# Output projection among the recurrence steps, with its sums in DRAM, in a one-layer hybrid decoder step

## The chip, the cores and the metric

The kernel runs on one core of one Trainium2 chip. The metric is the device time of one execution in microseconds (us). Times shown as "start" in rows of the trace count from the first instruction of the profiled execution.

## What is computed

One decoder layer for 1,024 prompt tokens and 8 decode tokens, width 1,024. The projected row is split: 512 channels go through a pooling mixer in 4 groups of 128, the rest through RWKV-7 with 8 heads of 64. Both results, side by side, go through one output projection.

```python
h = _rmsnorm(x, norm1_g)
proj = h @ w_in                                     # 1024 -> 512 + 1792
pool_out = _pool_mixer(proj[..., :512], ...)        # window means minus token, 128x128 map per group
# RWKV-7, per head, token by token:
sa = einsum('bhvk,bhk->bhv', S, -kk)
S = S * decay + sa (kk * a) + v k                   # state update
y = einsum('bhvk,bhk->bhv', S, r)                   # then group norm, bonus, gate
mix = concatenate([pool_out, rwkv_out]) @ w_out     # 1024 -> 1024
x = x + mix
h2 = _rmsnorm(x, norm2_g)
x = x + square(relu(h2 @ w_up)) @ w_down            # 1024 -> 4096 -> 1024
```

The final norm, the new states and the pooling and shift buffers are outputs too.

## The kernel before

**Layout.** Everything is transposed: channels on the 128 partitions, tokens along the free axis. The tokens stand in two halves (512, and 512 + 8 decode tokens); each half has two segments of 256. A full-precision product is made of three matmuls on split operands (`gemm`, L183): high by high, high by low, low by high. `weights` (L155) loads a weight tile `wr` on GpSimd's DMA queue (4 buffers) and splits it into `wh` and `wl` on ScalarE and VectorE (6 buffers each).

**Stages.** `token_block` builds the normed input of a segment (`xh`, `xl`, 2 buffers: segment 2 reuses those of segment 0). `project` makes one of 18 row blocks `pj` of the input projection: 0 to 3 are the pool groups, 4 to 15 r, k and v of the four head pairs, 16 and 17 the low-rank inputs. `stage1` (S) makes the chunk matrices of a head pair and half, and writes `sc`, `bkt`, `vt`. `inverse` (I) inverts the 64 by 64 chunk matrices of two head pairs over one segment, with two trips through DRAM (`blk`, `inv`, `Dg`, `TX`). `chain` (C) then steps the state through the segment's four chunks (`pcs`, L588 to L599), norms and gates the output (`py`, L622) and stores it to DRAM (`mix`). There are eight units S0 to S7 (four head pairs, two halves) and eight blocks I0 to I7 and C0 to C7: C0, C1 and C2, C3 are the first half, C4 to C7 the second.

**Pool groups.** `pools` (P) steps `pool_group`: the `pj` products of a group, window sums, then the 128 by 128 map `po` with a weight `pw` from the GpSimd queue. `pw` has one buffer, so that each load waits for the `po` of the group before. The result goes to `mix` in DRAM.

**Order.** The string `ORDER` is the program order: R makes r, k, v, T the token blocks of segments 2 and 3 with block 16's weights, L the second half's low-rank inputs, Q the decode pool rows, D the first part of `decode`. Within it the scheduler orders each engine's instructions by priority (`high_priority`, the LEAD offsets); each engine runs its list in order and waits on semaphores.

**Output projection.** `mixed` reads a `mix` tile back and splits it (`mr`, `mh`, `ml`); `out_block` makes 128 output channels (`mx`) and adds them to `x`. The first half's products are written behind C7 in the program, with priority ahead for C7 (`lead_chain(blocks[7])`), and the decode steps between them. The second half's follow with 7 of 8 k tiles, then `norm2(0)`, then the last k tile among the first `up` products. The MLP (`up`, `dn`) takes the rest.

## Time and profile before

| | |
|---|---|
| runs of before, us | 1369.88, 1372.07, 1374.78 (median 1372.07) |
| profiled execution, us | 1369.46 |
| its span, first to last instruction, us | 1367.7 |
| C0 starts / C7's last `py` / MLP's steady stretch starts, us | 127.3 / 555 / 647.6 |

The profiled execution spends 1.8 us outside its span. PE is TensorE's matmuls; they are pipelined, so the busy time of PE is longer than what it would need at the spacing of its matmuls, and only the spacing tells its load. PEclk is the clock that TensorE was granted, as a share of full speed.

### The profile page before, as it was taken

To read this page: it belongs to the slowest core of one execution; us is meant where nothing else is said; L and a number is where in the kernel's file an instruction comes from. 1 tells how busy PE (TensorE), PEld (TensorE's weight loads), DVE (VectorE), ACT (ScalarE), POOL (GpSimd) and SP (SyncE) were. 2 spreads that over 40 slices of the span, in tenths; PEclk is the share of its full clock that TensorE was granted. 3 is DMA by queue.
4 is the path that set the end of the run, shared out by engine and by line. 5 is a ranking of instruction groups with operands and counts; after the bars stand their busy time and mean duration, and the time that the engine had idled before them with its cause. 6 is when DMAs were issued, how large, how long until landed. Compare 5 with 4: busy or idle time off the path is not lost.

```text
span 1367.7 us, 24214 instructions
## 1 busy us (share of the span) xinstructions
PE 1304.4 (95%) x9748; PEld 1149.8 (84%) x9748; DVE 806.9 (59%) x1782; ACT 555.2 (41%) x1261; POOL 152.2 (11%) x301
## 2 busy tenths in 40 slices
PE   6999996999999899999999999999999999999996
PEld 6988775878877676798999999999999999999986
DVE  7887577747866765748644535445444354453447
ACT  7655766766767667626211212112111121121123
POOL 3112001111100110120010100100000100000000
PEclk9999996999999899999999999999999999999998
DMA  7234123221321542431111111111111111111103
GB/s 226 70 80 115 44 61 74 77 52 54 71 50 42 160 127 79 158 132 60 47 55 39 55 47 40 54 40 47 54 39 55 47 43 50 45 48 48 47 7 124
DMA packets 81647, 94.52 MB, mean 69 GB/s; under 512 B 52504, under 2 KB 58776, under 8 KB 81528
## 3 DMA queue, kind: packets, MB, share of 16 engines
q0 software_dynamic: 20480, 66.04, 15.1%
q1 hardware_dynamic: 59728, 25.10, 7.3%
q8 instruction: 76, 1.25, 0.4%
q10 hardware_dynamic: 1328, 1.85, 0.4%
q14 instruction: 35, 0.29, 0.1%
HBM read 79.67 MB, written 13.51 MB: 68 GB/s over the span
## 4 chain that ended last, share of the span: by engine, by line
PE 77%; ACT 7%; DVE 6%; issue 5%; DMA 3%; POOL 1%; SPq 0%; DVEq 0%; POOLq 0%; ACTq 0%
PE dn L183 26%; PE up L183 26%; PE pj L183 7%; PE mx L183 5%; PE sc L415 2%; PE pcs L599 1%; PE pcs L593 1%; ACT SV L100 1%; DMA cst<-in_consts 1%; ACT TT L100 1%; PE py L589 1%; DVE tm L517 1%; ACT ys L100 1%; PE pcs L588 1%; DVE wl L173 1%
## 5 line engine op out<-in xcount | busy, mean ns | idle before, releaser
L100 ACT ACTIVATE wh<-wr 128x512 fp32r<-128x512 f32 x230 | 143.2, 626 | 357.8 <-PE dn L183 276.2
L183 PE MATMUL up<-h2h,wl 128*128 128x260 f32 (+1 forms) x768 | 245.6, 320 | 0.0
L183 PE MATMUL up<-h2h,wh 128*128 128x260 f32 (+1 forms) x768 | 245.1, 320 | 0.5 <-DVE u L930 0.5
L183 PE MATMUL up<-h2l,wh 128*128 128x260 f32 (+1 forms) x768 | 244.9, 320 | 0.0
L183 PE MATMUL dn<-uh,wl 128*128 128x512 f32 (+1 forms) x720 | 231.0, 321 | 0.0
L183 PE MATMUL dn<-ul,wh 128*128 128x512 f32 (+1 forms) x720 | 230.6, 320 | 0.0
L183 PE MATMUL dn<-uh,wh 128*128 128x512 f32 (+1 forms) x720 | 230.3, 320 | 0.0
L969 DVE TENSOR_TENSOR x<-dn,x 128x260 f32<-128x260 f32 (+1 forms) x192 | 99.1, 516 | 189.6 <-PE dn L183 189.6
L183 PE MATMUL pj<-xh,wh 128*128 128x258 f32 (+3 forms) x576 | 174.8, 303 | 10.8 <-ACT wh L100 9.7
L173 DVE TENSOR_TENSOR wl<-wr,wh 128x512 fp32r<-128x512 f32 x230 | 156.4, 684 | 41.0 <-ACT wh L100 37.6
L183 PE MATMUL pj<-xh,wl 128*128 128x258 f32 (+3 forms) x576 | 172.0, 299 | 0.0
L183 PE MATMUL pj<-xl,wh 128*128 128x258 f32 (+3 forms) x576 | 171.6, 298 | 0.0
L183 PEld LDWEIGHTS up<-h2l,wh 128*128 128x128 f32 x768 | 144.5, 188 | 12.3 <-DVE h2l L912 0.6
L183 PEld LDWEIGHTS up<-h2h,wh 128*128 128x128 f32 x768 | 144.2, 188 | 11.7 <-DVE u L930 0.9
L183 PEld LDWEIGHTS up<-h2h,wl 128*128 128x128 f32 x768 | 144.4, 188 | 11.1
L183 PEld LDWEIGHTS dn<-ul,wh 128*128 128x128 f32 x720 | 135.5, 188 | 10.9 <-issue 0.2
L183 PEld LDWEIGHTS dn<-uh,wh 128*128 128x128 f32 x720 | 135.7, 188 | 10.5
L183 PEld LDWEIGHTS dn<-uh,wl 128*128 128x128 f32 x720 | 135.4, 188 | 10.6 <-issue 0.2
L100 ACT ACTIVATE uh<-u 128x260 fp32r<-128x260 f32 (+1 forms) x96 | 47.2, 492 | 238.6 <-DVE u L931 238.6
L183 PEld LDWEIGHTS pj<-xh,wh 128*128 128x128 f32 x576 | 112.4, 195 | 16.5 <-ACT wh L100 9.7
L930 DVE SCALAR_TENSOR_TENSOR u<-up,rs 128x260 f32<-128x260 f32 (+1 forms) x96 | 49.5, 517 | 120.8 <-PE up L183 114.3
L183 PEld LDWEIGHTS pj<-xl,wh 128*128 128x128 f32 x576 | 112.6, 195 | 3.9 <-issue 2.6
(291 smaller groups left out, 2088.5 us busy)
## 6 DMA issues: line engine op xcount, KB each, us to landing
wr<-in_w_in POOLq DMA_DIRECT2D x72, 256.0 KB, 3.1
wr<-in_w_up POOLq DMA_DIRECT2D x64, 256.0 KB, 2.9
wr<-in_w_down POOLq DMA_DIRECT2D x64, 256.0 KB, 2.9
wr<-in_w_out POOLq DMA_DIRECT2D x26, 256.0 KB, 3.3
xr<-in_xT SPq DMA_DIRECT2D x16, 256.0 KB, 3.7
mr<-mix SPq DMA_DIRECT2D x8, 260.0 KB, 3.5
x<-in_xT SPq DMA_DIRECT2D x2, 1040.0 KB, 7.9
blk<-AA SPq DMA_DIRECT2D x16, 128.0 KB, 2.6
```

The lines of the kernel that those rows point to most:

```text
L100: A.activation(out, in_, func, bias=bias, scale=scale, **k)
L173: V.tensor_tensor(l[:, :w], raw[:, :w], f32(h[:, :w]), op=ALU.subtract)
L183: PE.matmul(ps, lhs, rhs, start=i == 0, stop=i == n - 1)
L415: PE.matmul(scs[h][:, c, :], BK[R[h], c, :, :], AR[R[h], c, :, h, :], start=True, stop=True)
L517: V.tensor_tensor(pr[:, q], l[:, q].unsqueeze(2).to_broadcast([64, m, m, m]), r[:, q].rearrange("p k j -> p j k").unsqueeze(1).to_broadcas ...
L588: PE.matmul(pq[:, u], B.AR[u][:, c, 0, :, :], SV[:, c, u], start=True, stop=True)
L589: PE.matmul(py[u][:, c, :, :], SV[:, c, u], B.AR[u][:, c, 1, :, :], start=True, stop=False)
L593: PE.matmul(pa[:, u], TT[:, 4 * u + c, :, :], Q[:, u], start=True, stop=True)
L599: PE.matmul(pu[:, u], B.BKT[u][:, c, :, :], SV[:, c, u], start=True, stop=True)
L930: V.scalar_tensor_tensor(u, ps[:, :n], 0.0, rs2[:, cs], ALU.max, ALU.mult)
L969: V.tensor_tensor(d, ps[:, :n], d, op=ALU.add)
```

## The change

The program order is rewritten. Parts of the pool groups stand elsewhere, T preloads the weights of row blocks 16 and 17, `project_later` makes both blocks for segment 2 before segment 3 takes part, and four new parts M0 to M3 make output projection: M0 and M1 the whole first half (8 k tiles, right behind S7 and D), M2 and M3 the second half over k tiles 0 to 5. They take `x` from the input, add the product and store the sum to a DRAM tensor `x1_d`. Behind the loop `load_x1` reads all of it back, and the last two k tiles (C6's and C7's heads) are added behind `norm2(0)`.

```diff
-ORDER = """R0 S0 R1 S1 P00 I0 Q P01 C0 I1 P02 C1 R2 S2 R3 T S3 L I2 R4 C2 I3 R5 C3 S4 S5 I4 R6 C4 I5 R7 C5 S6 S7 I6 P10 C6 I7 P11 P12 D"""
+ORDER = """R0 S0 R1 S1 I0 Q R2 C0 I1 R3 P00 P01 P02 T C1 S2 L S3 I2 R4 C2 I3 P10 R5 C3 S4 S5 I4 R6 P11 C4 I5 R7 P12 C5 S6 S7 M0 I6 D M1 C6 I7 M2 M3 C7"""
...
-                GP.dma_start(raw.rearrange("p (m c) -> p m c", c=P), src)
+                GP.dma_start(raw.rearrange("p (m c) -> p m c", c=src.shape[-1]), src)
...
-        with tc.high_priority(offset=LEADX if b > 1 else 0):
+        with tc.high_priority(offset=LEADX if b == 2 else 0):
...
+    def project_later():
+
+        ws = [ahead.pop(m) for m in (16, 17)]
+        for b in (2, 3):
+            next(late.pop(b))
+            if b == 2:
+                next(late[3])
+            for w, (m, use) in zip(ws, hold):
+                project_block(m, w, b, use, 0)
+
+    hold = []
+
     def project(m, half, use):
+        if m > 15 and half:
+            hold.append((m, use))
+            return
...
+        if half:
+            project_later()
         sigm(z0[0:64, :n], z0[0:64, :n], 0.0, 2.0)
...
             next(late[2])
             ahead[16] = weights(I["w_in"][16])
-            next(late[3])
+            ahead[17] = weights(I["w_in"][17])
...
+    x1_d = [dr.tile([P, KT, n], F32, name=f"x1_{i}") for i, (_, n) in enumerate(HALF)]
+    mx = {}
+
+    def mixed_early(half):
+
+        mx[half] = []
+        n = HALF[half][1]
+        for k in range(KT - 2 * half):
+            if k % 4 == 0:
+                h, l = (xp.tile([P, KT, 266], F32R, tag=x, name=f"m{x}{k}_{half}", bufs=NX).rearrange("p k t -> p (k t)")
+                        for x in ("xh", "xl"))
+            c = slice(n * (k % 4), n * (k % 4) + n)
+            raw = big(f"mr{k}_{half}", ("f", "e", "u0", "u1")[k % 4])[:, :n]
+            SY.dma_start(raw, mix_d[k][half])
+            act(h[:, c], raw)
+            V.tensor_tensor(l[:, c], raw, f32(h[:, c]), op=ALU.subtract)
+            mx[half].append((h[:, c], l[:, c]))
+
+    def out_early(m, half):
+
+        c0, n = HALF[half]
+        ops = mx[half]
+        x = big(f"xm{m}_{half}", f"d{m % 2}")[:, :n]
+        SY.dma_start(x, I["xT"][:, m, c0:c0 + n])
+        w = weights(I["w_out"][m, :, :len(ops) * P])
+        for o, q in ((0, 260), (260, 260)) if half else ((0, 512),):
+            ps = ps_d.tile([P, 512], F32, tag="d", name=f"mx{half}_{m}_{o}")
+            gemm(ps[:, :q], w, [(h[:, o:o + q], l[:, o:o + q]) for h, l in ops])
+            V.tensor_tensor(x[:, o:o + q], ps[:, :q], x[:, o:o + q], op=ALU.add)
+        SY.dma_start(x1_d[half][:, m, :], x)
+
+    def outs(part):
+        half, part = part // 2, part % 2
+        if part == 0:
+            if half:
+                for _ in dec[0]:
+                    pass
+            mixed_early(half)
+        for m in range(4 * part, 4 * part + 4):
+            out_early(m, half)
+            if dec:
+                next(dec[0], None)
...
+        elif c[0] == "M":
+            outs(int(c[1]))
...
-            SY.dma_start(x1[half][:, k:k + 4, :], I["xT"][:, k:k + 4, c0:c0 + n])
+            SY.dma_start(x1[half][:, k:k + 4, :], x1_d[half][:, k:k + 4, :])
...
-    lead_chain(blocks[7])
-    open_x1(0)
-    with tc.tile_pool(name="opa", bufs=1, side="right", reuse_waits="tile") as op:
-        ops = [mixed(op, k, 0, NMA) for k in range(KT)]
-        for m in range(KT):
-            out_block(m, weights(I["w_out"][m]), ops, 0, 0, 512)
-            next(dec, None)
-    open_x1(1)
+    for half in range(2):
+        open_x1(half)
+        load_x1(half)
...
-        ops = [mixed(op, k, 1, 3) for k in range(KT - 1)]
-        for m in range(KT):
-            w = weights(I["w_out"][m, :, :(KT - 1) * P])
-            for o in (0, 260):
-                out_block(m, w, ops, 1, o, 260)
         norm2(0, 512, lambda x: op.tile([P, 512], F32, tag="n2", name=x, bufs=2))
-        last = [mixed(op, KT - 1, 1, 3)]
-        w7 = [w for m in (0, 4) for w in weights(I["w_out"][m:m + 4, :, (KT - 1) * P:].rearrange("m p c -> p m c"))]
-        for m in range(KT):
-            for o in (0, 260):
-                out_block(m, w7[m:m + 1], last, 1, o, 260)
+        ops = [mixed(op, k, 1, 3) for k in range(KT - 2, KT)]
+        for m in range(0, KT, 2):
+            w = weights(I["w_out"][m:m + 2, :, (KT - 2) * P:].rearrange("m p c -> p m c"))
+            for i in range(2):
+                for o in (0, 260):
+                    out_block(m + i, w[2 * i:2 * i + 2], ops, 1, o, 260)
```
```

Wide products (`pj`, `mx`, `up`) in the program order of PE between marks of the recurrence; "start" is a block's first `pcs`, "end" its last `py` with `glu`. The other matmuls are left out here.

| stretch of PE's order | before: 512 columns, 256 to 266 columns | after |
|---|---|---|
| program start to C0 start | 0, 649 | 0, 652 |
| C0 start to C1 start | 0, 82 | 0, 92 |
| C1 start to end | 0, 55 | 0, 80 |
| C1 end to C2 start | 0, 276 | 0, 418 |
| C2 start to C4 start | 0, 527 | 0, 441 |
| C4 start to C5 start | 0, 77 | 18, 45 |
| C5 start to end | 0, 53 | 30, 0 |
| C5 end to C6 start | 40, 9 | 141, 0 |
| C6 start to C7 start | 33, 0 | 3, 29 |
| C7 start to end | 41, 0 | 0, 74 |

**Between C1's end and C2's start, GpSimd's queue.** Before, the first half's last pool weights are loaded ahead of the recurrence's first `mix` stores (`pw` is a pool weight, `d` a pool group's result, `ys` the recurrence's output of block C0, `wr` a weight tile).

```order
L751 DMA pw1_0_1247<-in_pool_w 128x128
L776 DMA mix0_0_70<-d0_0_1106 128x512
L165 DMA wr_2349<-in_w_in 128x512
L751 DMA pw2_0_1558<-in_pool_w 128x128
L776 DMA mix1_0_72<-d1_0_1147 128x512
L165 DMA wr_2413<-in_w_in 128x512
L751 DMA pw3_0_1567<-in_pool_w 128x128
L776 DMA mix2_0_74<-d2_0_1409 128x512
L165 DMA wr_2419<-in_w_in 128x512
L399 MEMSET AA1_0_2202 128x16
L751 DMA pw0_1_5500<-in_pool_w 128x128
```

After the change the same loads stand behind C1's stores.

```order
L645 DMA mix4_0_78<-ys0_1_2422 128x256
L645 DMA mix5_0_80<-ys0_1_2422 128x256
L768 DMA pw1_0_2082<-in_pool_w 128x128
L793 DMA mix0_0_70<-d0_0_1941 128x512
L768 DMA pw2_0_2240<-in_pool_w 128x128
L793 DMA mix1_0_72<-d1_0_1982 128x512
L768 DMA pw3_0_2249<-in_pool_w 128x128
L793 DMA mix2_0_74<-d2_0_2091 128x512
L165 DMA wr_2310<-in_w_in 128x512
L165 DMA wr_2316<-in_w_in 128x512
L165 DMA wr_2322<-in_w_in 128x512
L165 DMA wr_2328<-in_w_in 128x512
L793 DMA mix3_0_76<-d3_0_2133 128x512
```

Three `pw` loads, each with a `mix` store of the group before it in line behind, now stand between C1's output and the next four weight loads, which are row blocks 16 and 17 of the second half.

**Between C5's end and C6's start, PE.** Before, the last `bkt` of S7 stands here, followed by `vt`, the start of C6's chunks, and the first pool maps (`po`) and output products (`mx`, of channels 0 and 1).

```order
L427 MATMUL bkt3_3_5193<-cst_86,BK_147 128x128 x4
L441 MATMUL vt1_2_5200<-cst_86,v2_1_4191 128x128 x2
L441 MATMUL vt1_2_5200<-cst_86,v3_1_4664 128x128 x2
L441 MATMUL vt1_3_5210<-cst_86,v2_1_4191 128x128 x2
L441 MATMUL vt1_3_5210<-cst_86,v3_1_4664 128x128 x2
L588 MATMUL pcs_108<-SV1_2_5199,AR0_135 128x128
L589 MATMUL py1_2_0_5517<-AR0_135,SV1_2_5199 128x128
L588 MATMUL pcs_108<-SV1_2_5199,AR1_136 128x128
L589 MATMUL py1_2_1_5518<-AR1_136,SV1_2_5199 128x128
L774 MATMUL po0_1_0_5905<-d0_1_5366,pw0_1_5500 128x256
L774 MATMUL po0_1_256_5908<-d0_1_5366,pw0_1_5500 128x264
L183 MATMUL mx0_0_0_8_6201<-mh0_0_6142,wh_6191 128x512
```

After the change the same `bkt` stands here, among the output products of channel block 4.

```order
L183 MATMUL mx0_4_0_5980<-mxh4_0_5572,wh_5976 128x512
L432 MATMUL sc3_3_0_5512<-AR3_138,BK_147 128x128 x4
L183 MATMUL mx0_4_0_5980<-mxl4_0_5573,wh_5976 128x512
L432 MATMUL sc3_3_1_5513<-AR3_138,BK_147 128x128 x4
L183 MATMUL mx0_4_0_5980<-mxh4_0_5572,wl_5977 128x512
L183 MATMUL mx0_4_0_5980<-mxh4_0_5572,wh_5976 128x512
L444 MATMUL bkt3_3_5528<-cst_86,BK_147 128x128 x4
L183 MATMUL mx0_4_0_5980<-mxl4_0_5573,wh_5976 128x512
L183 MATMUL mx0_4_0_5980<-mxh4_0_5572,wl_5977 128x512
L183 MATMUL mx0_4_0_5980<-mxh4_0_5572,wh_5976 128x512
L183 MATMUL mx0_4_0_5980<-mxl4_0_5573,wh_5976 128x512
L458 MATMUL vt1_2_5535<-cst_86,v2_1_4343 128x128 x2
```

Ahead of this `bkt` and behind C5's end there are now 64 products of 512 columns and all matmuls of S6 and S7, and behind it, up to C6's start, 77 (of before 0 and 40); the pool maps are gone from here.

**Behind C7, SP's queue.** Before, the second half's `mix` tiles are read, and then `x`, in two halves, from the kernel's input.

```order
L869 DMA mr2_1_6705<-mix2_1_75 128x520
L869 DMA mr3_1_6711<-mix3_1_77 128x520
L869 DMA mr4_1_6717<-mix4_1_79 128x520
L869 DMA mr5_1_6723<-mix5_1_81 128x520
L869 DMA mr6_1_6729<-mix6_1_83 128x520
L869 DMA mr7_1_7248<-mix7_1_85 128x520
L855 DMA x11_6672<-in_xT 128x4x520 x2
```

After the change `x` of both halves comes from the sums in DRAM.

```order
L869 DMA xm6_1_6917<-in_xT 128x520
L875 DMA x1_1_458<-xm5_1_6862 128x520
L869 DMA xm7_1_6972<-in_xT 128x520
L875 DMA x1_1_458<-xm6_1_6917 128x520
L919 DMA x11_7150<-x1_1_458 128x2080
L875 DMA x1_1_458<-xm7_1_6972 128x520
L919 DMA x10_7144<-x1_0_457 128x2048 x2
L919 DMA x11_7150<-x1_1_458 128x2080
```

The loads of `x1_1` and `x1_0` stand around and behind the store of the last sum (`xm7`), in the same queue.

## Rows read from the trace of the kernel before

**Rows 1.** The page's first part: busy time of each engine, its share of the span, and its instructions.

```profile
PE 1304.4 (95%) x9748; PEld 1149.8 (84%) x9748; DVE 806.9 (59%) x1782; ACT 555.2 (41%) x1261; POOL 152.2 (11%) x301
```

**Rows 2.** The table by stretches, cut at the marks of the recurrence: start and end, length, busy time (and instructions) of PE, its weight loads, DVE, ACT and POOL, the granted clock, the share of DMA time and GB/s.

```profile
0.00:127.30 127.30, 113.58 (x978) 103.65 (x978) 102.20 (x252) 81.16 (x175) 27.40 (x65) 0.99 0.44 127
127.30:158.90 31.60, 30.44 (x370) 24.68 (x369) 18.22 (x51) 21.88 (x57) 2.67 (x7) 1.00 0.27 66
158.90:185.10 26.20, 25.54 (x176) 21.16 (x175) 19.28 (x52) 18.71 (x44) 0.00 (x0) 1.00 0.01 2
185.10:261.30 76.20, 59.88 (x548) 52.63 (x546) 55.58 (x134) 50.77 (x120) 10.08 (x20) 0.82 0.34 88
261.30:292.10 30.80, 28.95 (x368) 24.26 (x368) 18.30 (x52) 20.62 (x57) 3.05 (x7) 1.00 0.22 57
261.30:393.50 132.20, 125.78 (x1198) 108.60 (x1198) 89.30 (x226) 84.67 (x209) 14.64 (x29) 0.97 0.23 60
393.50:428.50 35.00, 33.04 (x399) 27.43 (x399) 29.40 (x82) 23.56 (x64) 3.35 (x7) 1.00 0.19 50
428.50:454.30 25.80, 25.71 (x166) 20.59 (x165) 18.54 (x47) 19.28 (x45) 2.16 (x4) 1.00 0.12 30
454.30:494.30 40.00, 33.33 (x313) 26.14 (x312) 26.31 (x67) 24.95 (x66) 8.09 (x15) 0.77 0.60 170
494.30:529.80 35.50, 33.36 (x361) 23.68 (x359) 24.08 (x64) 28.76 (x95) 1.98 (x4) 0.97 0.34 106
529.80:556.00 26.20, 25.92 (x158) 19.26 (x158) 12.66 (x31) 15.18 (x47) 3.00 (x7) 1.00 0.19 61
```

**Rows 3.** The timeline of PE at some marks: start, duration, engine, line, tiles, shape and count; in brackets the wait before.

```profile
230.20 1.09 PE L427 MATMUL bkt<-cst,BK 128*128 128x128 f32 x4 [1.05 <-DVE AR L422]
...
261.34 0.71 PE L593 MATMUL pcs<-Q,TT 128*128 128x128 f32 x4
...
362.29 0.60 PE L427 MATMUL bkt<-cst,BK 128*128 128x128 f32 x4
...
393.46 0.71 PE L593 MATMUL pcs<-Q,TT 128*128 128x128 f32 x4
...
460.02 1.09 PE L427 MATMUL bkt<-cst,BK 128*128 128x128 f32 x4 [1.78 <-DVE AR L422]
...
494.27 1.05 PE L593 MATMUL pcs<-Q,TT 128*128 128x128 f32 x4
```

**Rows 4.** The same timeline in two steady stretches of output products, the first and last row of each: 21 matmuls of 512 columns, then 25 of 260; and two neighbouring `py` of four records.

```profile
560.16 0.40 PE L183 MATMUL mx<-mh,wh 128*128 128x512 f32 x1
...
564.79 0.40 PE L183 MATMUL mx<-mh,wl 128*128 128x512 f32 x1
...
587.29 0.28 PE L183 MATMUL mx<-mh,wl 128*128 128x260 f32 x1
...
590.17 0.28 PE L183 MATMUL mx<-mh,wl 128*128 128x260 f32 x1
...
555.04 1.13 PE L622 MATMUL py<-z,glu 128*128 128x256 f32 x4
555.83 0.58 PE L183 MATMUL mx<-mh,wh 128*128 128x512 f32 x1
```

**Rows 5.** PE's waits between 185 and 261: line, releaser, us in total, times, longest.

```profile
PE pb L384 <- DVE bv L382: 5.3, 1, 5.3
PE ss L250 <- DVE acc L234: 4.1, 1, 4.1
PE pk L373 <- ACT w L100: 3.1, 1, 3.1
```

**Rows 6.** POOL's waits in the same stretch, one row of its weight loads.

```profile
POOL wr L165 <- DVE acc L234: 9.6, 4, 4.4
```

**Rows 7.** The table by stretches again, for the granted clock (the number behind POOL's).

```profile
200.00:207.00 7.00, 6.89 (x25) 5.50 (x26) 4.32 (x12) 5.54 (x14) 0.54 (x1) 0.57 0.57 160
213.00:233.00 20.00, 12.72 (x53) 10.17 (x53) 15.27 (x39) 7.18 (x16) 2.15 (x4) 0.50 0.41 95
```

**Rows 8.** The timeline of POOL's queue, pool weights of the second half and the waits before them.

```profile
467.81 0.54 POOL L751 DMA_DIRECT2D pw<-in_pool_w  x1 [8.12 <-PE po L774]
...
472.97 0.54 POOL L751 DMA_DIRECT2D pw<-in_pool_w  x1 [2.98 <-PE po L774]
```

**Rows 9.** All instructions on the tile `pw`: time from issue to landing of its loads.

```profile
DMA to landing us min/median/max: 2.1/2.7/5.8
```

**Rows 10.** The chain that ended last, between 556 and 620: start, duration, work.

```profile
569.54 3.42 DMA mr<-mix
...
583.00 35.41 PE mx L183 x294
```

**Rows 11.** PE's waits between 556 and 648.

```profile
PE mx L183 <- DVE x L880: 1.4, 1, 1.4
PE ss L905 <- DVE acc L903: 0.7, 1, 0.7
```

**Rows 12.** DMA between 555 and 600: GB/s in 40 slices, and issues with count, KB each and the median us to landing.

```profile
GB/s 0 25 259 197 37 145 7 7 144 375 401 202 3 109 257 383 310 59 207 125 323 374 348 403 412 399 382 211 15 0 0 227 181 0 0 98 258 52 15 0
...
mr<-mix SPq DMA_DIRECT2D x8, 260.0 KB, 3.5
x<-in_xT SPq DMA_DIRECT2D x2, 1040.0 KB, 7.9
```

More of the change, by code (lines that the diff above doesn't have):

```diff
@@ L850, in open_x1, with load_x1 @@
     def open_x1(half):
-        c0, n = HALF[half]
+        n = HALF[half][1]
         xq = open_pool(ctx, f"x1{half}", side="right", reuse_waits="tile")
         x1.append(xq.tile([P, KT, n], F32, name=f"x1{half}"))
+    def load_x1(half):
         for k in range(0, KT, 4):
-            SY.dma_start(x1[half][:, k:k + 4, :], I["xT"][:, k:k + 4, c0:c0 + n])
+            SY.dma_start(x1[half][:, k:k + 4, :], x1_d[half][:, k:k + 4, :])
     def x1s(m, c, n):
```

## The prediction

> **What bounds the kernel now.** I began with the page's engine shares: matmuls are busy for 95% of the span, VectorE for 59%, ScalarE for 41% [rows 1]. Busy time of pipelined matmuls says little, so I next read the spacing: 21 products of 512 columns start 4.63 us apart from first to last, 0.231 us each, and 25 of 260 columns 2.88 us, 0.120 us each [rows 4]. Two 256-column matmuls with plain fp32 operands, four records, take 555.04 to 555.83, 0.40 us each [rows 4]; I scale the recurrence's and the inverse's other matmuls from that by width (an estimate). The table by stretches [rows 2] then shows how long each stage takes, and the table of counts in the change's section what PE must do in it. The difference is what I call stall: time above PE's spacing, whether it shows as a wait, as half clock or as gaps of an in-order queue.
>
> | stretch | length before | wide + other work before | stall before | work after |
> |---|---|---|---|---|
> | to C0 | 127.3 | 77.9 + 26.3 | 23.1 | 78.2 + 22.9 |
> | C0 to C1 | 31.6 | 9.8 + 15.1 | 6.7 | 11.0 + 12.5 |
> | C1 | 26.2 | 6.6 + 16.6 | 3.0 | 9.6 + 10.5 |
> | C1 end to C2 | 76.2 | 33.1 + 14.4 | 28.7 | 50.2 + 26.6 |
> | C2 to C4 | 132.2 | 63.2 + 46.7 | 22.3 | 52.9 + 45.9 |
> | C4 to C5 | 35.0 | 9.2 + 18.5 | 7.3 | 9.6 + 16.8 |
> | C5 | 25.8 | 6.4 + 16.8 | 2.6 | 6.9 + 15.8 |
> | C5 end to C6 | 40.0 | 10.3 + 13.9 | 15.8 | 32.6 + 23.5 |
> | C6 to C7 | 35.5 | 7.6 + 18.6 | 9.3 | 4.2 + 16.2 |
> | C7 | 26.2 | 9.5 + 13.1 | 3.6 | 8.9 + 10.5 |
>
> Two kinds of stage stand side by side. C1, C5 and C7 take 25.8 to 26.2 us whatever fills them, C0 to C1 and C2 to C3 31.6 and 30.8 [rows 2]: a chain of small steps sets them. The others are set by a queue, or by the inverse. From the last `bkt` that an inverse needs to its chain's first `pcs` run 230.20 to 261.34, 362.29 to 393.46 and 460.02 to 494.27: 31.1, 31.2 and 34.3 us [rows 3].
>
> **The change part by part.** PE's matmuls are the same in sum (the two extra weight tiles load and split elsewhere), so a gain can only be stall that goes. The terms, each "before minus after".
>
> *To C0.* The pool maps' waits go, but C0's inverse stands with 3 us less work in its way; I take a loss of 1.5. Bounds: the work lost and one `pw` landing, 2.7 [rows 9], say -5 to +2.
>
> *C1 end to C2.* Before, PE is left waiting for VectorE and ScalarE by 5.3, 4.1 and 3.1 us [rows 5], the weight queue behind the token blocks that hold its buffers by 9.6 [rows 6], and the clock is 0.57 in one stretch of 7 us and 0.50 in one of 20 [rows 7], after such waits. Up to the last `bkt`, 45 of the 76.2 us pass for 22.8 us of work, and 31.1 follow. After the change 54.7 us of PE's order stand before that `bkt` and 22.0 behind it, so the second part still costs 31 (the inverse's latency), with 9 of stall. In the first part the row blocks 16 and 17 have their weights ready, and the products of segment 2 cover the chain of norms of segment 3. New is the run of three `pw` loads in the POOL rows of the order. Each is held until the `po` before it has read the one buffer, then lands in 2.7 [rows 9]: some 3.3 us with the `po` itself, 10 in all, with nothing but one group's products between them. The norm wait of 4.1 remains once. That is 14; I take 13, since some `pj` rows lie between, and the stage becomes 54.7 + 13 + 31 = 98.7, stall 22.0, gain **6.7**. Bounds: all three loads hidden and full clock, stall 10, gain 19; loads at 5.8 [rows 9] and another 20 us at half clock [rows 7], stall 37, loss 8.
>
> *C2 to C4.* C4's inverse still follows its last `bkt` by 31 us with 22.8 us of work in it (23.1 before), so its stall stays; C3's chain gets 2 us more work. Gain **1.6**, bounds 0 to 4. This stage loses 11 us of work and its length must fall with it; S4 and S5 are its VectorE load, which at 89.3 of 132.2 us [rows 2] leaves room.
>
> *C5 end to C6.* Before, 5.7 us pass to the last `bkt` and 34.3 behind it, for 20.5 us of work. PE waits for `pw` loads there (the queue sat 8.12 and 2.98 before two of them [rows 8]) and the clock goes to half; these go, since the pool groups of the second half now stand between C3 and C5. But they sat inside the 34.3, which the inverse sets. What counts is that S6, S7 and 64 wide products, 24.3 us of work, now come before that `bkt`, and 31.7 us stand behind it, instead of 20.5. The stage becomes 24.3 + 34.3 plus the two waits ahead of `bkt` that S7 had and S6 now has as well. One is the 1.78 of [rows 3]; I take 2.4 for all. So 61.0, stall 4.9, gain **10.9**. Bounds: 58.6 (gain 13.3), and 66 if stores, `x` loads and the decode steps in SP's queue delay the inverse's round trips by a landing of 3.5 [rows 12] or two (gain 6).
>
> *The stages that a chain sets.* They keep their length if the work in them was never the limit. They then lose the cover that the change takes out: 1.4 (C0 to C1), 3.1 (C1), 1.3 (C4 to C5), 0.5 (C5), 3.2 (C7), 9.5 in all. If the fill was part of their length, they lose nothing. I know no row that tells it, as all had about 23 us of work; I take half, a loss of **4.8** (bounds 0 and 9.5). C6 to C7 loses 5.8 of work, but its 35.5 us had the decode's first steps in it, against 30.8 of C2 to C3 [rows 2]; 4.7 comes back, loss **1.1**.
>
> *Behind C7.* Before, one `mix` tile is late by 3.42 [rows 10], and the waits of 1.4 and 0.7 follow [rows 11]. The 294 products then run 35.41 us without a gap [rows 10]. The round trip of C7's `mix` now lies under the rest of M3, some 186 products or 22 us. What comes instead is the return of `x1`: 4.2 MB in four loads, the last behind the last sum's store. Two loads of 1,040 KB landed 7.9 us after issue [rows 12], so four take about 15.8, less if the queues reach the 412 GB/s of the best slice in the same row. Cover is 96 products (11.5 us) and the first `up` of 24 (5.5 us), but the 96 may not be added into `x1` until its first part is there, and PSUM holds a few of them only. I take 8.5 of stall against 6.5 before (3.42, 2.1 and 1 of small waits), a loss of **2.0**; bounds +3 and -8. The DMA page of the Trainium skill ("DMA: Bandwidth & Descriptors", Specifications) gives 435 GB/s as the ceiling of the 16 engines; by it alone the return would be an estimated 9.6 us plus a landing, and this term about +1. The row for a pair shows little over half of that rate, so the sum goes by the row.
>
> *Sum.* -1.5 + 6.7 + 1.6 + 10.9 - 4.8 - 1.1 - 2.0 = +9.8. The MLP behind is the same code on the same tiles. Against the profiled execution, 1369.5, that gives 1359.7. The median of the runs is 2.6 above it, so **1362**.
>
> **The rivals.**
>
> *A. As worked out*, near 1362, and between 1352 and 1368 with the small terms at their bounds.
>
> *B. The pool loads do not show, and the clock holds.* The T stage gains 19 instead of 6.7: 1350. For it: POOL has nothing else to do there. Against: one `pw` buffer.
>
> *C. The cover moves and nothing more.* The chain stages lose all 9.5 and the T stage gains 2: 1371. For it: lengths of 25.8 to 26.2 that hardly differ [rows 2]. This is also the case in which the change doesn't do what it says: the first half's output products were already partly among the recurrence before (114 of 192 by the table of counts), so that only places are exchanged.
>
> *D. The return of `x1` stalls the first `up`.* All four loads serial at 7.9, behind the last store: 8 us worse than A: 1370. For it: the SP rows of the order.
>
> *E. Slower: the T stage at half clock.* It now holds 76.8 us of work between two chains. If the three `pw` waits bring the clock to 0.50 for 40 us, as 20 us were before [rows 7], the work done in them falls by 20 us, and the time is 1378 to 1382. It decides from about 14 us more stall than A has there. For it: 0.57 and 0.50 after waits of 3.1 to 5.3 us [rows 5, 7]. The Trainium skill ("TensorE: Matmul & The Clock Gate", Part 1) says that the throttled state is the default and that only activity releases it, which the trace bears out in that stage. Against: products of segment 2 stand between the loads.
>
> **How the numbers follow.** A 0.36, B 0.16, C 0.14, D 0.10, E 0.15; 0.09 is left for mishaps of SP's queue between C5 and C6 on the slow side. A measurement of this kernel tells some 0.3% (4 us) from no change, so 1368 and 1376 are the limits. A and B are faster, 0.52; C and D within it, 0.24; E and the rest slower, 0.24. The range leaves one in ten at each end: 1344 (B with the C5 stage's upper bound) to 1382 (E).
>
> **What would show it.** Right: C1's end to C2 near 99 us, C5's end to C6 near 61, C7 still 26, and the C6 inverse starting 26 us behind C5's end. Wrong: the granted clock below 0.8 in the T stage for longer than before; `pw` waits over 3.3 us; PE waiting over 8 us for `x1`; any chain stage longer than its length before.

## The result, and the profile after

The changed kernel takes 1385.39 us (median; 1384.88 to 1389.31), the one before 1372.93 in the same session: a ratio of 1.0115, interval 1.0084 to 1.0145. It is slower by 12.5 us in the medians and by 15.8 in the ratio, where 10 us less was forecast. The profiled execution took 1384.88, 15.4 more than before's, and that is the difference explained below.

The page's first part, as [rows 1]:

```profile
PE 1307.7 (95%) x9748; PEld 1148.1 (83%) x9748; DVE 808.4 (58%) x1784; ACT 554.7 (40%) x1263; POOL 154.0 (11%) x303
```

The same number of matmuls, 95% again: busy time tells nothing of 15 us. The table by stretches, cut at the marks of the recurrence, columns as [rows 2]:

```profile
0.00:121.60 121.60, 107.46 (x965) 99.05 (x965) 96.14 (x237) 81.05 (x169) 24.03 (x57) 1.00 0.44 125
152.40:175.10 22.70, 21.95 (x159) 19.07 (x157) 10.32 (x31) 10.69 (x31) 0.23 (x2) 1.00 0.10 25
175.10:284.50 109.40, 93.94 (x754) 80.08 (x753) 87.25 (x205) 69.96 (x164) 18.46 (x35) 0.86 0.34 95
463.80:526.50 62.70, 61.05 (x467) 43.91 (x465) 43.75 (x104) 40.92 (x124) 7.10 (x13) 0.97 0.48 135
526.50:561.70 35.20, 29.63 (x361) 23.60 (x361) 21.65 (x59) 24.49 (x72) 2.70 (x5) 0.88 0.30 84
585.70:700.30 114.60, 98.95 (x649) 90.18 (x648) 74.07 (x152) 48.62 (x97) 14.74 (x26) 0.93 0.36 122
```

The lines are: start to C0; C1; C1's end to C2 (the T stage); C5's end to C6; C6 to C7; C7's end to the first `dn`. The same last stretch before:

```profile
556.00:684.80 128.80, 125.55 (x842) 114.28 (x841) 89.01 (x182) 58.92 (x117) 19.69 (x36) 1.00 0.32 102
```

Before, PE is busy in all but 3.3 us of it; after, 15.7 are idle and the clock is 0.93, though it is shorter. For each stage I took its length less all its matmuls at their spacing (0.231 and 0.120 us, the others by width, as in the prediction) from both traces. "Gain" is that stall before minus after:

| stage | predicted gain | measured | stall before, after |
|---|---|---|---|
| to C0 | -1.5 | +2.7 | 24.1, 21.4 |
| T stage | +6.7 | **-4.7** | 27.1, 31.8 |
| C2 to C4 | +1.6 | +4.7 | 19.0, 14.3 |
| C5's end to C6 | +10.9 | +7.9 | 18.3, 10.4 |
| five stages that a chain sets | -4.8 | -3.4 | 21.0, 24.4 |
| C6 to C7 | -1.1 | **-6.4** | 6.9, 13.3 |
| C7's end to first `dn` | -2.0 | **-16.5** | 6.8, 23.3 |
| sum (with 0.2 from the MLP) | +9.8 | -15.5 | |

Three terms failed, by 11.4, 5.3 and 14.5 us; the others together are 6 better than worked out. The stalls before are counted anew here, from the trace, and differ from the prediction's, which counted the program order (27.1 for 28.7, 19.0 for 22.3, 18.3 for 15.8, 6.9 for 9.3); a gain can't be read closer than these 2 to 3 us.

### The profile page after: what moved, and what is told of

Its sections match the earlier page's. It is cut to its first block, busy times and chain, and to the rows that moved or that the text cites. A ratio compares the mean times of both kernels' runs of the same rounds, so it can differ in the third digit from the quotient of the medians.

```text
span 1383.1 us, 24301 instructions
## 1 busy us (share of the span) xinstructions
PE 1307.7 (95%) x9748; PEld 1148.1 (83%) x9748; DVE 808.4 (58%) x1784; ACT 554.7 (40%) x1263; POOL 154.0 (11%) x303
## 4 chain that ended last, share of the span: by engine, by line
PE 77%; DMA 6%; ACT 6%; DVE 6%; issue 3%; POOL 1%; SPq 0%; DVEq 0%; ACTq 0%; POOLq 0%
PE dn L183 26%; PE up L183 26%; PE pj L183 8%; PE mx L183 4%; PE sc L432 3%; DMA inv<-Es 1%; DMA TX<-inv 1%; PE pcs L616 1%; PE pcs L610 1%; ACT SV L100 1%; DVE tm L534 1%; PE py L606 1%; DMA wr<-in_w_in 1%; ACT TT L100 1%; ACT ys L100 1%
## 5 line engine op out<-in xcount | busy, mean ns | idle before, releaser
L100 ACT ACTIVATE wh<-wr 128x512 fp32r<-128x512 f32 x232 | 143.3, 623 | 347.1 <-PE dn L183 276.2
L183 PE MATMUL up<-h2h,wh 128*128 128x260 f32 (+1 forms) x768 | 246.2, 321 | 0.7 <-DVE u L988 0.7
L183 PE MATMUL up<-h2h,wl 128*128 128x260 f32 (+1 forms) x768 | 246.4, 321 | 0.0
L183 PE MATMUL up<-h2l,wh 128*128 128x260 f32 (+1 forms) x768 | 246.1, 321 | 0.0
L183 PE MATMUL dn<-uh,wl 128*128 128x512 f32 (+1 forms) x720 | 230.9, 321 | 0.0
L183 PE MATMUL dn<-ul,wh 128*128 128x512 f32 (+1 forms) x720 | 230.6, 320 | 0.0
L183 PE MATMUL dn<-uh,wh 128*128 128x512 f32 (+1 forms) x720 | 230.3, 320 | 0.0
L183 PE MATMUL pj<-xh,wh 128*128 128x258 f32 (+3 forms) x576 | 172.3, 299 | 12.5 <-ACT wh L100 9.7
L183 PE MATMUL pj<-xl,wh 128*128 128x258 f32 (+3 forms) x576 | 169.2, 294 | 0.0
L183 PE MATMUL pj<-xh,wl 128*128 128x258 f32 (+3 forms) x576 | 168.7, 293 | 0.0
L183 PEld LDWEIGHTS up<-h2h,wh 128*128 128x128 f32 x768 | 145.0, 189 | 12.9 <-DVE u L988 1.9
L183 PEld LDWEIGHTS up<-h2l,wh 128*128 128x128 f32 x768 | 145.3, 189 | 12.4 <-DVE h2l L970 0.4
L183 PEld LDWEIGHTS up<-h2h,wl 128*128 128x128 f32 x768 | 145.2, 189 | 11.3 <-issue 0.2
L183 PEld LDWEIGHTS dn<-ul,wh 128*128 128x128 f32 x720 | 135.5, 188 | 10.9 <-issue 0.2
L183 PEld LDWEIGHTS dn<-uh,wh 128*128 128x128 f32 x720 | 135.7, 188 | 10.5
L183 PEld LDWEIGHTS dn<-uh,wl 128*128 128x128 f32 x720 | 135.4, 188 | 10.6 <-issue 0.2
L100 ACT ACTIVATE uh<-u 128x260 fp32r<-128x260 f32 (+1 forms) x96 | 47.2, 492 | 237.5 <-DVE u L989 237.5
L183 PEld LDWEIGHTS pj<-xh,wh 128*128 128x128 f32 x576 | 110.3, 192 | 16.9 <-ACT wh L100 10.3
L183 PEld LDWEIGHTS pj<-xl,wh 128*128 128x128 f32 x576 | 110.3, 192 | 3.9 <-issue 2.6
```

The source lines that it names most:

```text
L100: A.activation(out, in_, func, bias=bias, scale=scale, **k)
L183: PE.matmul(ps, lhs, rhs, start=i == 0, stop=i == n - 1)
```

## Experiments

Theory 1: the tail. The second half's projection returns late from DRAM, and this costs 16. Theory 2: the T stage, by its pool weights. Rival: the two big edits fight, or only one of them is bad. Ratios are to the kernel before, with 95% intervals. "Stall" is worked out as in the table above.

### Which half of the change costs

**e1**, the new order alone; the output projection stands behind the loop as before.

```diff
-... P12 C5 S6 S7 M0 I6 D M1 C6 I7 M2 M3 C7"""
+... P12 C5 S6 S7 I6 C6 I7 D"""
```

> The kernel before with the new program order, project_later and the preloaded weights of row blocks 16 and 17, but with no output projection in the loop: both halves' products and x stand behind it as before. Theory 'return' (the loss sits behind C7, where the sums come back from DRAM): C1 end to C2 about 108 us as in the changed kernel, stall behind C7 near the 6.5 of before, 1366 to 1375 in all. Rival 'order' (the new order itself costs it, through the T stage and the chains with less cover): 1380 or more.

Measured 1402.88, 1.0246 (1.0221 to 1.0271). C5's end to C6:

```profile
465.90:528.20 62.30, 48.12 (x378) 33.78 (x376) 39.63 (x97) 39.89 (x117) 3.26 (x6) 0.75 0.36 94
```

It is as long as after's 62.7, with 31 us of work in place of 52, at a clock of 0.75. The order puts S6 and S7 late, and their inverse waits for them: S6's first product starts at 376.0 before (ahead of C4), at 426.5 after and at 432.0 here (26 us behind C4's start in both). That makes a hole, whatever fills it. So theory 'return' alone is refuted. Nor is the stall behind C7 near 6.5 without any return of sums: it is about 13 here.

**e5**, the projection alone, in the order of before.

```diff
-... R7 C5 S6 S7 I6 P10 C6 I7 P11 P12 D"""
+... R7 C5 S6 S7 P10 P11 P12 M0 I6 D M1 C6 I7 M2 M3 C7"""
```

> The other half of the change alone: the order of before up to C5, T and L as before, and the four parts of output projection in the loop (the second half's pool groups go ahead of M0, which takes their input buffers). Theory 'return' (behind C7 the sums' way through DRAM costs about 17 us of stall more than before, whatever the order): C5's end to C6 40 to 46 us, stall behind C7 20 to 26, 1378 to 1390 in all. Theory 'late S' (the new order alone is bad, since pool groups ahead of S2 and S6 push these back and lay the inverses bare; the projection in the loop is good): stall behind C7 under 12, 1355 to 1372.

Measured 1403.45, 1.0232 (1.0207 to 1.0257). There the projection comes too late for C6, as the pool groups run first (41.0 us with 17 of work), and lands behind C7:

```profile
450.60:491.60 41.00, 30.03 (x289) 22.34 (x288) 22.74 (x59) 21.86 (x58) 6.48 (x12) 0.66 0.56 156
564.00:716.80 152.80, 130.57 (x831) 117.54 (x830) 91.72 (x187) 61.69 (x134) 19.00 (x34) 0.89 0.38 123
```

The last line holds 114 us of work and 38.6 of stall: all of M2's and M3's products stand behind C7, and no longer beside a recurrence. PE's longest waits there:

```profile
PE ss L946 <- DVE acc L944: 8.5, 2, 6.7
PE mx L183 <- ACT mxh L100: 7.2, 1, 7.2
PE mx L183 <- DVE x L926: 4.4, 1, 4.4
```

The first and the last are those of the sums' return, and after has them at the same size (8.4 and 4.2, below): they don't hang on the order. The time lies beyond both theories' ranges. So each edit alone costs over 30 us, and together 12.5: the order makes a hole and the projection fills it.

**e2**, M0 and M1 only (second half behind C7 as before), and **e4**, with M2 but without M3:

```diff
-... M0 I6 D M1 C6 I7 M2 M3 C7"""
+... M0 I6 D M1 C6 I7 C7"""      # e2
+... M0 I6 D M1 C6 I7 M2 C7"""   # e4
```

> The changed kernel without M2 and M3: only the first half's projection runs in the loop, the second half's stands behind it as before, with x read from the input. Theory 'return': stall behind C7 back to 6 to 9 us from 23.7, but C7 loses 9 us of cover, so 1374 to 1381. Rival 'order': the stall behind C7 changes by under 5 us, and the time is 1385 or more, since C7 loses its cover.

> The changed kernel without M3: channel blocks 0 to 3 of the second half run early over six k tiles as in M2, blocks 4 to 7 stand behind the loop over all eight k tiles, with x from the input, and cover the return of blocks 0 to 3 and of the first half. Theory 'return': stall behind C7 6 to 10 us instead of 23.7, C6 and C7 as in the changed kernel, 1368 to 1374 in all. Rival 'order': 1382 or more.

e2 measured 1400.02, 1.0222 (1.0198 to 1.0245); e4 1388.45, 1.0143 (1.0117 to 1.0168). In e2 C7 has 17.0 us of stall in place of 4.5 and C6 to C7 19.7 in place of 13.3: M2 and M3 are wanted as cover there. Behind C7 some 13 us of stall are left of after's 23.3, where theory 'return' wanted 6 to 9, and what is gained there is lost again ahead of it. In e4 the tail is no better (stall 25.4), since the `mix` tiles are late now:

```profile
PE mx L183 <- ACT mh L100: 16.5, 3, 7.3
```

### The tail

**e8** is e4 with the `mix` reads ahead of the read of the second half's sums (`load_x1(0)` stays ahead of them):

```diff
-    SY.dma_start(x1[1][:, 0:4, :], x1_d[1][:, 0:4, :])
     load_x1(0)
...
+        ops.append(mixed(op, KT - 1, 1, 3))
+        SY.dma_start(x1[1][:, 0:4, :], x1_d[1][:, 0:4, :])
```

> The kernel without M3 again (e4), with the reads in another order in SP's queue: the mix tiles of the second half and the first half's sums ahead of the read of channel blocks 0 to 3 of x1_1, which waits for the last store. In e4 the mix tiles stood behind that read, and PE waited 16.5 us for them. Theory 'return': stall behind C7 7 to 12 us instead of 25.4, 1368 to 1376 in all. If VectorE's two norms are what the stretch behind C7 waits for: 1382 or more.

1387.59, 1.0116 (1.0100 to 1.0132): the wait is 14.4 instead of 16.5. This doesn't show that the order of the reads is not what holds them: the two reads of `load_x1(0)` now wait for the last sum's store themselves, and three `mix` reads stand behind them in the queue as before (start, duration of issue):

```profile
594.55 0.32 SPq L875 DMA_DIRECT2D x<-xm  x1
594.92 3.21 SPq L932 DMA_DIRECT2D mr<-mix  x3
603.83 0.80 SPq L919 DMA_DIRECT2D x<-x  x2
605.61 1.63 SPq L932 DMA_DIRECT2D mr<-mix  x3
```

**e3** gives the sums four buffers in turn, not two:

```diff
-        x = big(f"xm{m}_{half}", f"d{m % 2}")[:, :n]
+        x = big(f"xm{m}_{half}", ("d0", "d1", "f", "e")[m % 4])[:, :n]
```

> The changed kernel with the tiles that take x and the sum (xm) in four buffers instead of two, so that a load of x doesn't wait for the store of the sum two places before. Theory 'return' in its first form (the two buffers pace M3: store, load, add, one after the other): the 233 products behind C7 lose 4 to 8 of their 10.3 us of stall, 1377 to 1382 in all. In its second form (only the last store and the four reads behind it count): the last product of M3 ends earlier by under 2 us, 1383 to 1386. Rival 'order': 1385.

1385.13, 1.0114 (1.0084 to 1.0144), stall 24.1: not the sums' buffers.

What does hold the tail? After's SP queue at C7's end (start, duration of issue):

```profile
610.81 0.32 SPq L919 DMA_DIRECT2D x<-x  x1
611.70 0.32 SPq L875 DMA_DIRECT2D x<-xm  x1
617.59 1.27 SPq L919 DMA_DIRECT2D x<-x  x3
```

The first row reads part of the second half's `x1`, the second row stores the last sum. The next three reads, the two of the first half's `x1` in front, start 5.9 us later; the waits name that store's landing:

```profile
SPq L919 <- DMA x<-xm: 5.5, 1, 5.5
```

And PE waits behind C7 for

```profile
PE ss L963 <- DVE acc L961: 8.4, 2, 6.7
PE mx L183 <- DVE x L943: 4.2, 1, 4.2
PE mx L183 <- DVE xm L874: 2.3, 3, 1.7
```

with three stretches of the table that tell why `ss`, the sum of squares of `norm2`, comes late:

```profile
610.00:620.00 10.00, 5.52 (x33) 5.11 (x32) 4.05 (x9) 2.88 (x6) 1.08 (x2) 0.72 0.76 245
620.00:640.00 20.00, 20.00 (x134) 18.37 (x133) 19.35 (x40) 16.89 (x33) 0.54 (x1) 0.97 0.37 155
652.00:662.00 10.00, 2.22 (x5) 1.08 (x6) 5.45 (x13) 5.19 (x13) 0.00 (x0) 0.67 0.00 1
```

First `x1` is missing; when it is there, `norm2` of the first half and the last k tiles' additions are due at once and VectorE is busy for 19.35 of 20 us; `norm2` of the second half comes behind them, and PE stands for most of 10. Before, `norm2(0)` ran under the 294 products [rows 10] and `ss` waited 0.7 [rows 11].

**e7** moves the first half's pool groups ahead, as before had them (it is the base of the next runs, and bears on theory 2 as well):

```diff
-ORDER = """R0 S0 R1 S1 I0 Q R2 C0 I1 R3 P00 P01 P02 T C1 ...
+ORDER = """R0 S0 R1 S1 P00 I0 Q P01 R2 C0 I1 R3 P02 T C1 ...
```

> The changed kernel with the first half's pool groups where they stood (P00 behind S1, P01 behind Q, P02 ahead of T), the rest as changed. Theory 'late S': S2's first product comes 10 us or more earlier after C1's start, C1's end to C2 falls from 108 to 85 to 98 us, stall there 22 to 27 instead of 32, 1376 to 1382 in all. If the token blocks alone set that stage: 104 us or more and 1383 to 1388.

1371.34, 1.0008 (0.9994 to 1.0023): 14 us better than after, with the tail unchanged (115.6 us, stall 24.3).

**e11** is e7 with `x` read from the input, not from the sums, so that no read depends on the last store's data.

```diff
-            SY.dma_start(x1[half][:, k:k + 4, :], x1_d[half][:, k:k + 4, :])
+            c0, n = HALF[half]
+            SY.dma_start(x1[half][:, k:k + 4, :], I["xT"][:, k:k + 4, c0:c0 + n])
```

> e7 with the four reads behind the loop taken from the kernel's input instead of from the sums (the products of M0 to M3 are made and stored, but left out of the output). It takes away the wait of the reads for the stores and keeps their bytes, their place and the memory that they wait for. If the stores' landing is what costs: stall behind C7 falls by 4 to 8 us, 1363 to 1367. If memory and the queue's order are: within 2 us of e7, 1369 to 1373.

1372.72, 1.0012 (0.9994 to 1.0031). The tail is as it was:

```profile
PE ss L964 <- DVE acc L962: 8.4, 2, 6.7
```

So it isn't the data: the reads wait for the last sum's store (5.7 us there) without reading what it wrote. **e10** is e7 with the SBUF places of the two halves of `x1` exchanged, the reads still written in the same order.

```diff
-    x1 = []
+    x1 = [None, None]
...
-        x1.append(xq.tile([P, KT, n], F32, name=f"x1{half}"))
+        x1[half] = xq.tile([P, KT, n], F32, name=f"x1{half}")
...
-    for half in range(2):
+    for half in (1, 0):
         open_x1(half)
+    for half in range(2):
         load_x1(half)
```

> e7 with the two x1 tiles opened in the other order, so that the first half's tile stands in other memory and its reads are released by other instructions. Theory 'return': the first half's sums, stored 50 us earlier, are read at the last product of M3 and not behind the last store; its norm runs 6 us earlier; stall behind C7 17 to 21 instead of 24.3, 1364 to 1369. If it is the second half's last reads that count: 1370 to 1373.

1364.40, 0.9964 (0.9946 to 0.9981): 0.4% faster than before, the only version clear of it on that side, in one session. SP's queue, and PE's waits:

```profile
595.62 0.32 SPq L919 DMA_DIRECT2D x<-x  x1
596.51 0.32 SPq L875 DMA_DIRECT2D x<-xm  x1
596.88 6.55 SPq L919 DMA_DIRECT2D x<-x  x3
```

```profile
PE up L183 <- ACT h2h L100: 4.5, 1, 4.5
PE mx L183 <- DVE xm L874: 3.1, 3, 2.1
PE ss L964 <- DVE acc L962: 1.3, 1, 1.3
```

The two reads of the first half's `x1` are now the first row and the first of the last: 26 and 27 us after C7's end instead of both at 32. The wait for the store is still in the queue, inside the last row, and has moved to the second half's reads behind them. The wait of `ss` goes from 8.4 to 1.3, one for `up`'s operand takes part of it back, and the stall falls by 5.5, from 24.3 to 18.8. So what delayed the first half's `x1` was the memory it was given: whichever half lies there waits for the last sum's store to land.

**e14** makes the same exchange in the changed kernel itself, with its order.

> The changed kernel with nothing but the other order of opening the two x1 tiles (the edit of e10 without the first pool groups' move). If the two losses are independent, the one behind C7 and the one of the order: stall behind C7 from 23.3 to 18 or so, as e7 to e10, and 1378 to 1381 in all. If the gain of e10 needed e7's order: 1384 to 1387.

1385.74, 1.0099 (1.0064 to 1.0134). Here too the tail's stall falls by 5.2 (to 18.1), but the way to C0, T, and C3 to C4 gave 2.2, 1.5 and 1.8 back in its profile; the four runs spread over 11 us, so this doesn't show a gain of the whole: the 5 us behind C7 were gained in both orders, the faster time only in e7's.

**e13** is e10 with the stores of the sums on GpSimd's queue (`GP.dma_start`).

> e10 with the sums stored from GpSimd's queue instead of SP's, where the inverse's trips through DRAM, the decode's states and the reads of x stand. If the place in SP's queue is what lengthens the stages from C5's end to C7 (58.5 and 33.0 us in e10): these fall by 3 to 6 us together, and 1358 to 1362 in all. If the transfers themselves collide, or the weights behind the stores in GpSimd's queue come late instead: 1364 to 1370.

1370.46, 1.0005 (0.9989 to 1.0020): 6 us worse than e10; C6 to C7 has 2.3 us more stall, and the tail 1.9.

### The T stage and the pool groups

**e15**, the changed kernel with three buffers for `pw`, meant to let the loads go ahead of the `po` before them:

```diff
-        pw_sb = pp.tile([P, P], F32, tag="pw", name=f"pw{g}_{half}")
+        pw_sb = pp.tile([P, P], F32, tag="pw", name=f"pw{g}_{half}", bufs=3)
```

> The changed kernel with three buffers for the pool weights instead of one, so that the weights of groups 1 and 2 are there before T. The prediction's term (three loads in a row behind one buffer, 10 us): C1's end to C2 falls from 108.4 to 98 to 102 us, 1376 to 1380 in all. If what PE waits for there are VectorE's window sums (6.1 us by the changed kernel's waits, none by the weights): C1's end to C2 stays within 2 us, 1383 to 1387.

1380.85, 1.0100 (1.0062 to 1.0138). The T stage takes 108.2 instead of 108.4 (by the start of the last `py`, plus 1.0). But the edit didn't move the loads: they stand at the same places of GpSimd's queue, behind C1's stores and 3.7 and 3.9 us apart. The second and third of them, in after and in e15:

```profile
183.01 0.54 POOL L768 DMA_DIRECT2D pw<-in_pool_w  x1 [2.50 <-PE po L791]
186.94 0.54 POOL L768 DMA_DIRECT2D pw<-in_pool_w  x1 [2.85 <-DVE d L776]
186.72 0.54 POOL L768 DMA_DIRECT2D pw<-in_pool_w  x1 [2.50 <-PE po L791]
190.61 0.54 POOL L768 DMA_DIRECT2D pw<-in_pool_w  x1 [2.81 <-DVE d L776]
```

So e15 says nothing of what the loads cost; after's own rows do. What PE waits for in its T stage:

```profile
PE po L791 <- DVE d L785: 6.1, 2, 3.3
PE pb L401 <- DVE bv L399: 4.7, 2, 4.4
```

Both are VectorE's results, the pool groups' window sums and the end of `stage1`'s chain of small steps. The two loads landed at 185.0 and 189.0, the sums of their groups were done at 185.4 and 189.8, and VectorE was busy from the first sum to the last:

```profile
182.40:189.80 7.40, 1.42 (x6) 0.68 (x4) 7.10 (x15) 2.61 (x7) 2.68 (x5) 0.86 0.24 89
```

So PE waited for the sums. The loads were there only 0.4 and 0.9 us earlier, and with faster sums PE would have met them next. With these waits the clock falls, as it did before [rows 7]:

```profile
190.00:200.00 10.00, 10.00 (x31) 6.31 (x32) 4.58 (x8) 6.30 (x13) 2.70 (x5) 0.60 0.73 223
210.00:220.00 10.00, 8.39 (x37) 6.84 (x36) 8.92 (x23) 2.88 (x8) 0.54 (x1) 0.50 0.09 12
220.00:230.00 10.00, 8.98 (x33) 6.77 (x34) 6.94 (x17) 7.85 (x16) 2.16 (x4) 0.57 0.40 124
```

**e16**, the same in e10: 

> e10 with the same three buffers. With the first half's groups 0 and 1 early, two loads remain in T: 1360 to 1363 if the loads cost there, 1363 to 1366 if the window sums do.

1370.81, 1.0005 (0.9988 to 1.0021): T 101.5 against 102.6, lost again elsewhere; here too the loads in T issue where they did (184.5 and 188.4 against 184.2 and 188.3). In e7 and e10, where the maps of two of the four pool groups are left in T, the stage has 27.4 and 28.0 of stall instead of 31.8.

**e17** is e10 with S2 ahead of the third segment's work:

```diff
-... P01 R2 C0 I1 R3 P02 T C1 S2 L S3 I2 ...
+... P01 R2 C0 I1 S2 R3 P02 T C1 L S3 I2 ...
```

> e10 with S2 ahead of R3 and T instead of behind C1, so that its first product comes before C1's start as in the kernel before (in e10 34 us behind it). Theory 'late S' (pool groups and token blocks ahead of S2 lay that stretch bare): C1's end to C2 falls from 102.6 to 85 to 95 us, with stall 20 to 25 instead of 28, 1355 to 1361 in all. If the token blocks' weights and VectorE set the stretch: its stall stays within 2 us, 1363 to 1368.

1369.49, 0.9981 (0.9963 to 1.0000). The T stage itself gains most of any run:

```profile
183.30:272.20 88.90, 78.55 (x706) 72.89 (x705) 67.14 (x160) 58.41 (x141) 16.26 (x31) 0.90 0.39 109
```

Its stall is 20.4 instead of 28.0, and some 6 us of products leave the stage with S2. S2's first product starts at 153.1 before, at 191.7 after, 188.3 in e10 and 144.7 here: in this order an early S2 is worth 7.6 us of stall. It isn't what after lost against before, though: before had 27.1 with an early S2, and e7 and e10 come to that with a late one. But the other stages take back 10 us, C6 to C7 4.5 and C4 to C5 2.7 of them, through the order that the scheduler then finds; which rule does it I haven't traced.

**e18** is e17 with S6 behind R6, ahead of C4, and S7 behind C5. It doesn't compute the layer: S6 writes its chunk matrices into buffers (`ARs` and its fellows, four for all units) that C4 has still to read. So its time, 1377.8, 1.0049 (1.0027 to 1.0071), is that of no working order; in it C5's end to C6 takes 30.5 us, with 4.8 of stall, and more comes back, 24 us from C2 to C4 and 27 behind C7.

**e6** puts the second half's pool groups behind S7, as e5 has them, in the new order.

```diff
-... I3 P10 R5 C3 S4 S5 I4 R6 P11 C4 I5 R7 P12 C5 S6 S7 M0 ...
+... I3 R5 C3 S4 S5 I4 R6 C4 I5 R7 C5 S6 S7 P10 P11 P12 M0 ...
```

> The changed kernel with the second half's pool groups P10 to P12 behind S7 instead of between C3 and C5; the first half's as changed. Theory 'late S': S6 starts ahead of C4 again (26 us behind it in the changed kernel), C5's end to C6 falls from 62.8 to 38 to 46 us, and C6's start comes 20 us or more earlier. With 'return' holding too, the output products only move behind C7 and the whole is 1376 to 1386; if 'late S' is all of the loss, 1360 to 1372.

1398.20, 1.0192 (1.0175 to 1.0209). C5's end to C6 shrinks to 39.1, the projection comes late, and behind C7 stand 38.2 us of stall, as in e5. In both orders tried, the projection costs most where it ends behind the recurrence.

### Decode

**e9** is e7, **e12** e10, each with `D` ahead of M0 (`S6 S7 D M0 I6 M1 C6`).

> e7 (first half's pool groups early) with D ahead of M0 instead of behind I6, so that the decode ends earlier, M2 can start earlier, and M3 ends nearer to C7's end. Theory 'return': the stall behind C7 (24.3 in e7) falls by 5 to 12 us, because x1 returns under C7's own latency, 1359 to 1367 in all. If the place of the return doesn't matter (ScalarE's and VectorE's norms do): 1369 to 1373.

> e9 and e10 together. Theory 'return': the gains add in part, 1354 to 1364. If neither wait matters: 1369 to 1373.

1372.72, 1.0017 (1.0000 to 1.0034) and 1369.26, 0.9995 (0.9978 to 1.0012). C6 to C7 got longer in both (36.7 and 36.9 against 33.1 and 33.0), and the stall behind C7 stayed within 1 us of e7's and e10's: an earlier decode gave nothing there.

## Why the prediction was wrong, by its own steps

**Behind C7: -2.0 predicted, -16.5 measured, the largest miss.** The step that failed is "I take 8.5 of stall", worked out from "Cover is 96 products (11.5 us) and the first `up` of 24". The return was sized about right: the reads of 1,040 and 1,024 KB landed 8.3 and 6.7 us after their issue, against the 7.9 I used (each the median of two reads, not the time of a pair). But the price isn't the landing. Worked out from the matmuls' starts, the 23.3 us of stall stand in three places. M3, which I counted as free cover, lost only 2.8 in its 184 products behind C7. The next 49 products, those of the last k tiles, took 12.8 us for 5.9 of work: 4.2 of that is the wait for `x1`, and the clock stood at 0.50 from 614 to 621. The remaining 13 to 14 stand behind the first `up`. That part I had put at nothing: `norm2(0)`, hidden under 294 products before, moves behind the return, meets VectorE's additions and pushes back `norm2` of the second half, for which `ss` waits. e10 prices the memory place at 5.5 us of the whole. Rival D named the return and the right stage, but as a wait of the first `up` and with 8 us; the rows above hold 8.4 for `ss`, which e10 brings to 1.3 by an earlier `x1`.

**T stage: +6.7 predicted, -4.7 measured.** The step that failed is the 13 in "54.7 + 13 + 31 = 98.7", the waits up to the last `bkt`. The two parts took 82.5 and 26.9:

```profile
175.10:257.60 82.50, 69.03 (x392) 56.92 (x392) 68.33 (x156) 53.43 (x121) 14.03 (x26) 0.81 0.30 90
257.60:284.50 26.90, 24.91 (x365) 23.16 (x363) 18.93 (x50) 16.52 (x43) 4.42 (x9) 1.00 0.43 110
```

The second part is better than I said, with 3.0 of stall for the 9 I took. The first has the work I said (54.2 us), but 28.3 of stall where I took 13. I named the `pw` loads as the new wait; in the rows above PE waits for VectorE's sums in their place, and VectorE is busy for 68.3 of the 82.5 us. I counted no time at half clock, and the clock was at 0.50 (1.2 GHz) for 31 us, 27 before [rows 7]. What after lost against before is the pool groups' place: with them early (e7) the stall is 27.4. That it is their sums on VectorE, and not their other work, is argued from the waits; no run took out the sums alone. Rival E named this stage and half clock, but priced 14 to 20 us more stall than A. The stage has 9.8 more, and only 3.4 us more at half clock than before. The Trainium skill ("TensorE: Matmul & The Clock Gate", Part 1) has the throttled state as the default that activity releases; the rows agree: the clock fell within a wait of PE of 3.3 us (to 189.91) and at the end of one of 4.4 (to 208.32). Rival B, that the pool loads don't show, was right about the loads and wrong about the clock.

**C6 to C7: -1.1 predicted, -6.4 measured.** The step that failed is "4.7 comes back": I let the stage shrink to the 30.8 of C2 to C3, as "the decode's first steps" would leave it. It took 35.2, as before (35.5), with 22 us of work in place of 29. Decode didn't leave it: the chain of after goes through `dS`, `dT` and `dW` at 531 to 534. At its end, where mostly the small matmuls of the inverse and of the chain are left, the clock falls:

```profile
546.50:556.50 10.00, 7.68 (x150) 4.80 (x148) 4.15 (x11) 5.86 (x16) 1.70 (x4) 0.82 0.44 129
556.50:561.70 5.20, 3.62 (x71) 3.13 (x71) 1.76 (x3) 4.72 (x12) 0.46 (x1) 0.50 0.16 54
```

In e1, without M0 to M3 and with `D` last, the same stage takes 31.3, stall 3.9; in e7, with `D` where after has it, 33.1, stall 8.3. So the decode's place is not all of it, and how the 6.4 divide between decode, thinner cover and clock stays open.

**C5's end to C6: right in kind.** 61.0 forecast, 62.7 measured, though the work is only 52 us: the stage is set by S7's last `bkt` and the inverse behind it, as the step has it. In part the two errors cancel. The way to that `bkt` took 24.4 without the 2.4 of waits that I added to 24.3, and the second half took 38.3 instead of 34.3: from the `bkt` at 488.2 to 526.5. The gain is 7.9 instead of 10.9, on a stall before that is counted as 18.3 and not 15.8. One piece of it stands in the chain that ended last, `TX`, the inverse's second trip through DRAM:

```profile
508.83 7.94 DMA TX<-inv
```

The same read landed in 5.1 before, and in 3.8 in e7, where the same path takes 32.9. Its issue is 1.2 and 1.7 us behind an `x1` store and a state store; in e7 one `x1` store stands 0.6 us ahead, so a store close by alone doesn't do it. The Trainium skill ("DMA: Bandwidth & Descriptors", Queues, rings and completion order) says that a transfer's completion signal lands only after every earlier write of the same DMA engine; these two rows fit that only in part, and no run here tested it.

**The stages that a chain sets**: half of the cover was a guess (-4.8; measured -3.4). The fill turned out to be part of C1's length: it is 22.7 now, 3.5 less than before, with less work in it. Not all did so: C4 to C5 took 36.8 instead of 35.0, one of the signs of being wrong that I had named. **To C0** gained 2.7 instead of losing, and **C2 to C4** gained 4.7 instead of 1.6. Of the range, the lower end isn't the sum it names: B with the C5 stage's bound gives 1347, not 1344.

**What stays open.** The first pools' place is worth 14 us of the whole (e7), of which the T stage holds 4.4 of stall, C5's end to C6 2.7, C4 to C5 4.2 and C6 to C7 5.4. Why the later stages gain from an edit 200 us ahead of them, beyond that the scheduler's lists differ there, I couldn't show. And of the tail's 16.5, e10 recovers 5.5; 11 stay.

## What to carry to other kernels

Don't price a moved piece of work alone: ask what it covered in the place it leaves and what will cover it where it goes (here the reorder and the projection each cost over 30 us alone and 12.5 together). When data returns through DRAM, look at which memory the return lands in: a tile on top of buffers that are still being stored waits for the store, and exchanging two tiles took 5 us of stall out of the tail in both orders tried, and 6 us (by the ratios) out of the whole in one of them. And before a one-buffer load is priced as a wait, look what else its reader waits for: PE waited 10.8 us in that stage for VectorE's results. When an edit changes nothing, look first whether it moved anything: three buffers left the loads where they were.

## What the runs showed of the hardware

The clock fell while PE was at work: over the 15 us at C6's end it was 0.82 in the mean and then 0.50, where PE was busy for 11.3 us, mostly with small matmuls, after 20 us at 1.00. And one read of 256 KB at the same place in the program took 5.1, 7.9, 3.8 and 5.0 us to land (before, after, e7, e10), a spread as large as most terms of the sum.
